# A transpose of the identity ahead of each run of products by weights, in a two-layer decoder trunk

## The chip, the cores and the metric

The kernel runs on one core of a Trainium2 chip. The metric is the device time of one execution in microseconds (us), lower is better; the time of a kernel is the median of its runs. A core has five engines with a queue each: TensorE (PE in the profile; its weight loads stand apart as PEld), VectorE (DVE), ScalarE (ACT), GpSimd (POOL) and SyncE (SP), which here only issues transfers. TensorE writes its results to PSUM, eight banks of which the kernel uses as one pool.

## The reference

The model is a decoder trunk of two layers over 256 tokens of width 2048. Each layer has a token mixer and a SwiGLU feed-forward network (FFN). Layer 0 mixes by retention with 8 heads, layer 1 by a short gated convolution. Cut to what matters here:

```python
for i in range(DEPTH):                                  # DEPTH = 2
    mod = (c_act @ w_mod[i] + b_mod[i])[:, None, :]
    sh1, sc1, g1, sh2, sc2, g2 = jnp.split(mod, 6, axis=-1)
    h = rms_norm(x, norm1_g[i]) * (1.0 + sc1) + sh1
    y = retention_mixer(h, ...) if i == 0 else short_conv_mixer(h, ...)
    x = x + g1 * y
    h = rms_norm(x, norm2_g[i]) * (1.0 + sc2) + sh2
    a, b = jnp.split(h @ ffn_w_in[i], 2, axis=-1)       # 2048 -> 2 x 5632
    x = x + g2 * ((silu(a) * b) @ ffn_w_out[i])         # 5632 -> 2048
return rms_norm(x, final_g)
```

Nearly all the arithmetic is in products of 256 tokens by weight matrices in 32-bit floats, 7296 tiles of 128 x 128 weights in all.

## The kernel before

**Splitting.** A 32-bit number is carried as two parts, `hi` (the number cast to the type `fp32r` that TensorE multiplies quickly) and `lo` (what the cast left out). A product of weights by activations is made of three terms: `hi` by `hi`, `hi` by `lo` and `lo` by `hi`. The activations lie in SBUF with both parts side by side, 2 x 256 columns, so that one matmul by `hi` weights does two terms.

**Weights.** They lie in one array in the order of use. Each transfer (`fetch`) brings 128 x 2048 numbers, 1 MB. `prepare` splits a half of that, 1024 columns or eight tiles of 128: ACT casts `hi` (L323), DVE subtracts to get `lo` (L326). Four such halves have room. `take` hands out the next tile and prepares up to two halves ahead.

**Products.** Most tiles pass through `product` (L356 to L374). For each tile it issues a pair: a 512-wide matmul of `hi` by both parts of the activations (L368), and a 256-wide one of `lo` by the upper part (L371). In each group all tiles of a column add up in one bank. 5396 pairs run in all: 496 in the retention's output (`rm` in the profile), the others in the FFNs and the convolution (`h` on the way in, `mid` on the way out). `packed` (L376) uses three 256-wide matmuls per tile, `tokens` (L402 to L420) 512-wide ones with the activations as the stationary side; both are used in the retention, `packed` also for the last column of an `output`.

**Order.** TensorE's queue has the order in which the code is written (a manual schedule). A scheduler places the instructions of DVE and ACT, outside the opening, by priorities. The stages on TensorE are: the retention's projections and heads, with the two halves of its output (`ret_out`) after four heads each; then FFN 0, the convolution, FFN 1. `normed` opens each of these last three: it works on six columns with 258-wide matmuls (L552 to L554) while the norm is computed. Then runs of `product` follow without a break, the input columns and `output` (L576) for the way out. In an FFN two such rounds come one after the other, 1994 pairs between `normed` and the last, `packed` column; in the convolution 912 pairs.

**Asides.** The last head before each `ret_out` leaves two pieces of work for later: `outputs` (nine 512-wide matmuls, L918) after 6 tiles, and `turned` (eight transposes of 128 x 128, L937) after 26 more or as soon after as the tiles of a row allow. They fall among the first pairs of `ret_out`.

Of the kernel before, what the change touches and what calls it, by code (L numbers as in the profile page):

```python
# [17 lines left out]
P = 128  # L18
# [28 lines left out]
MOST = 0.045  # L47
MOD_PRIO = -300
STEPS = (6, 26)
RAW_BUFS = 3  # L50
PART_BUFS = 4
ROW_AT = 64
# [146 lines left out]
def trunk(ctx: ExitStack, tc: tile.TileContext, x_in, c_in, pos_in, w_mod, cols_in, tab_in, w_all, out):  # L199
    nc = tc.nc  # L200
# [7 lines left out]
    def name(s):  # L208
        serial[0] += 1
        return f"{s}_{serial[0]}"  # L210

    def tmp(tag, shape=(P, S), dtype=F32, pool=work, bufs=None):
        return pool.tile(list(shape), dtype, tag=tag, name=name(tag), bufs=bufs)
# [24 lines left out]
    inv_freq, ident = tab[:, 0:1], tab[:, 1 : 1 + P]  # L238
# [7 lines left out]

    def mod_raw(t, pool=wpool, bufs=RAW_BUFS):
        raw = pool.tile([P, CHUNK], F32, tag="raw", name=name("raw"), bufs=bufs)
        nc.sync.dma_start(raw, w_mod[t])
        return raw  # L250
# [29 lines left out]
    def paced(n):  # L280

        units[0] += n
        due = 0
        for (a, i), (b, j) in zip(plan_mod, plan_mod[1:]):
            if units[0] >= a:
                due = min(j, i + (units[0] - a) * (j - i) // (b - a))
        allowed[0] = min(allowed[0] + n * MOST, 2.0) if n <= 64 else 0.0
        while todo and n_mod - len(todo) < due and allowed[0] >= 1.0:
            allowed[0] -= 1.0
            modulation(*todo.pop())  # L290

    def needed(layer, which, last=KT - 1):
        while any(m[:2] == (layer, which) and m[2] <= last for m in todo):
            modulation(*todo.pop())
# [7 lines left out]
    def fetch():  # L302
        raw = wpool.tile([P, CHUNK], F32, tag="raw", name=name("raw"), bufs=RAW_BUFS)
        nc.sync.dma_start(raw, w_all[n_fetched[0]])
        n_fetched[0] += 1
        fetched.append(raw)

    def prepare(between=None):
# [5 lines left out]
        if i == 0:  # L314
            if not fetched:
                fetch()
            raws[:] = [fetched.pop(0)]
            while first <= units[0] < early and len(fetched) < RAW_BUFS - 1 and n_fetched[0] < w_all.shape[0]:
                fetch()
# [11 lines left out]
    def take(group, k, col, width=P):  # L331

        assert order.pop() == (group, k, col, width)
        i = taken_cols[0] % HALF
        if i == 0:
            if ready and taken_cols[0]:
                ready.pop(0)
            while len(ready) < 1 + AHEAD * (units[0] >= first):
                n = len(ready)
                prepare()  # L340
                if len(ready) == n:
                    break
        taken_cols[0] += width
        return [t[:, i : i + width] for t in ready[0]]

    def bank():
        return ps.tile([P, 2, S], F32, tag="bank", name=name("bank"))

    asides, since = [], [0]

    def ticked(n):

        since[0] += n
        if asides and since[0] >= asides[0][0]:
            asides.pop(0)[1]()
            since[0] = 0  # L356

    def product(g, act, base=0, before=None, banks=None, last=True):

        fresh = not banks  # L360
        banks = banks or [bank() for _ in g.cols]
        for k in g.ks:
            if before:
                before(k)
            h = act[k - base]
            for c, pt in zip(g.cols, banks):
                hi, lo = take(g, k, c)
                nc.tensor.matmul(  # L368
                    pt, hi, h, start=fresh and k == g.ks[0], stop=False, skip_group_check=True
                )  # L370
                nc.tensor.matmul(  # L371
                    pt[:, 1, :], lo, h[:, 0, :], start=False, stop=last and k == g.ks[-1], skip_group_check=True
                )
            ticked(len(g.cols))  # L374
        paced(len(g.cols) * len(g.ks))
        return banks  # L376
# [87 lines left out]
    def norm_sums(accs):  # L464

        pt = bank()
        for i, acc in enumerate(accs):
            for t in range(2):
                nc.tensor.matmul(
                    pt[:, 0, t : t + 1], acc[:, t * P : (t + 1) * P], ones[:, 0:1],  # L470
                    start=i + t == 0, stop=i == len(accs) - 1, skip_group_check=True,
                )
        return pt

    def norm_roots(pt, n):

        r = tmp("rs", (P, 2), bufs=4)
        nc.vector.tensor_scalar(r, pt[:, 0, 0:2], 1.0 / n, EPS, op0=ALU.mult, op1=ALU.add)
        r2 = tmp("rs", (P, 2), bufs=4)
        nc.gpsimd.tensor_tensor(r2, r, half, op=ALU.pow)  # L480
        return r2
# [27 lines left out]
    def modulated(h, j, rb, layer, norm):  # L509
        shifted(h, scaled(j, rb, layer, norm), j, layer, norm)  # L510
# [18 lines left out]
    def normed(accs, layer, norm, g):  # L529

        needed(layer, SH2 if norm else SH1)
        shift = mod_s[layer][norm].unsqueeze(2).to_broadcast([P, KT, 2])
        ends = [h_open[:, :, i, S:] for i in range(2)]
        nc.scalar.copy(ends[0], shift)
        nc.vector.tensor_tensor(ends[1], shift, ends[0].bitcast(F32), op=ALU.subtract)
        banks = [bank().rearrange("p a b -> p (a b)")[:, : S + 2] for _ in g.cols]  # L540
        made = [0]

        def more(n):
            while made[0] < n:
                modulated(h[made[0]], made[0], root, layer, norm)
                made[0] += 1

        for k in g.ks:
            rows = [h_open[:, k, i, :] for i in range(2)]
            for c, pt in zip(g.cols, banks):  # L550
                hi, lo = take(g, k, c)
                nc.tensor.matmul(pt, hi, rows[0], start=k == 0, stop=False)  # L552
                nc.tensor.matmul(pt, hi, rows[1], start=False, stop=False)  # L553
                nc.tensor.matmul(pt, lo, rows[0], start=False, stop=k == KT - 1)  # L554
            if k == ROOTS_AT:
                r = norm_roots(norm_sums(accs), D)
            elif k == SPREAD_AT:
                root = tmp("rb", bufs=1)
                nc.scalar.copy(root, norm_spread(r))
            elif k > SPREAD_AT:  # L560
                more(min(k, made[0] + 2))
        more(KT)
        paced(len(g.cols) * len(g.ks))

        def total(pt, dst=None):
            end = tmp("end", (P, 1), bufs=2)
            nc.scalar.copy(end, pt[:, S : S + 1])
            t = tmp("low", bufs=3)
            nc.vector.tensor_tensor(t, pt[:, :S], root, op=ALU.mult)
            dst = tmp("sum", bufs=4) if dst is None else dst  # L570
            nc.scalar.activation(dst, t, AF.Identity, bias=end)
            return dst

        return [lambda dst=None, pt=pt: total(pt, dst) for pt in banks]

    def output(groups, act, which, last, after=None, base=None):  # L576

        layer, gate = which[0], mod_g[which[0]][which[1] == GT2]
        first, *groups = groups
        base, acc = first.ks[0] if base is None else base, None  # L580
        banks = product(first, act, base, last=False)
        for j, g in enumerate(groups):
            needed(*which, j)
            col = gate[:, j : j + 1]
            if last and j == KT - 1:
                (pt,) = packed(g, act, base)
                nc.vector.scalar_tensor_tensor(x[j], pt[:, 0, :], col, x[j], op0=ALU.mult, op1=ALU.add)
                acc = [acc, squares(None, x[j], "acc1")]
                if after:
                    after(j)  # L590
                return acc
            (pt,) = product(g, act, base, banks=banks[j : j + 1])
            t = tmp("sum", bufs=4)
            nc.vector.scalar_tensor_tensor(t, pt[:, 1, :], col, x[j], op0=ALU.mult, op1=ALU.add)
            nc.vector.scalar_tensor_tensor(x[j], pt[:, 0, :], col, t, op0=ALU.mult, op1=ALU.add)
            if last:
                acc = squares(acc, x[j])
            if after:
                after(j)


    with ExitStack() as inner:
# [70 lines left out]
        fresh = set()  # L673

        with tc.tile_pool(name="start", bufs=1) as sp:
# [57 lines left out]
            with tc.manual_schedule(engines={mybir.EngineType.DVE, mybir.EngineType.Activation}):  # L733
# [58 lines left out]
                banks = [bank() for _ in range(8)]  # L792

                def before(k):
                    low = []
                    prepare(lambda: low.append(row(k)))
                    low[0]()
# [109 lines left out]
        def mixed(head, both, v, sg):  # L907
# [36 lines left out]

            return list(zip(STEPS, [outputs, turned]))

# [39 lines left out]
    def sums(g):  # L986
        (pt,) = product(g, h)
        return lambda dst=None: summed(pt, dst)
# [108 lines left out]
```

## Time and profile before

| | us |
|---|---|
| Median of 3 runs | 2659.72 (2659.34 to 2661.05) |
| The profiled execution | 2657.39 |
| Its span | 2655.50 |
| Chain that ended last: PE | 76% of the span |
| Chain that ended last: "issue" | 20% of the span |
| DMA: read from HBM | 682.99 MB, 258 GB/s over the span |

The profile is of one execution. A group of instructions has a count, a total busy time and a mean duration. TensorE's matmuls are pipelined: a new one starts before the recorded end of the one before it. The recorded 399 ns of an L368 and 281 ns of an L371 therefore add up to more than the time that a pair takes, which has to be read from the starts. "Issue" in the chain of work is time for which the profile shows nothing that the engine waited for.

### The profile page before, as it was taken

How to read it: one execution, taken by the hardware profiler on the slowest of the kernel's cores; microseconds unless marked ns; L12 is line 12 of the kernel's file. 1: busy time of each engine (PE TensorE's matmuls, PEld its weight loads, DVE VectorE, ACT ScalarE, POOL GpSimd, SP SyncE). 2: the span in 40 equal slices, each digit the busy share in tenths (PEclk: the TensorE clock that was granted, in tenths of full speed). 3: DMA queues.
4: the chain of work that ended last, by engine and by line, in shares of the span. 5: the costliest groups of instructions: out<-in, count | busy, mean ns of one | idle time of the engine just before them, and what ended most of it. 6: DMA issues, size and time to landing. Idle time of an engine off the chain costs nothing.

```text
span 2655.5 us, 38222 instructions
## 1 busy us (share of the span) xinstructions
PE 2623.5 (99%) x15220; PEld 2298.5 (87%) x15220; DVE 1988.7 (75%) x2526; ACT 1245.2 (47%) x1755; POOL 148.3 (6%) x230
## 2 busy tenths in 40 slices
PE   7999999999999999999999999999999999999998
PEld 5998889888899888888888898888988888888887
DVE  7988878787798777777777888888886665555554
ACT  5545443444455444344444454444554443444443
POOL 0000001110000011101000001100000000000000
PEclk9999999999999999999999999999999999999999
DMA  9976668787687777777777768777676665555553
GB/s 398 401 270 242 238 232 319 267 301 263 244 301 260 295 285 271 279 276 280 273 279 262 279 214 328 276 276 257 254 278 247 252 222 183 183 190 190 181 185 126
DMA packets 96950, 687.58 MB, mean 259 GB/s; under 512 B 10753, under 2 KB 12545, under 8 KB 13825
## 3 DMA queue, kind: packets, MB, share of 16 engines
q1 hardware_dynamic: 96194, 684.48, 70.0%
q8 instruction: 119, 1.95, 0.3%
q10 hardware_dynamic: 576, 0.66, 0.1%
q14 instruction: 61, 0.50, 0.1%
HBM read 682.99 MB, written 2.10 MB: 258 GB/s over the span
## 4 chain that ended last, share of the span: by engine, by line
PE 76%; issue 20%; DVE 2%; DMA 1%; ACT 0%; SPq 0%; POOL 0%; POOLq 0%; ACTq 0%; DVEq 0%
PE bank L368 35%; PE bank L371 18%; PE bank L406 4%; PE bank L407 4%; PE bank L408 4%; PE bank L393 1%; PE bank L392 1%; PE bank L391 1%; PE bank L553 1%; PE bank L552 1%; PE bank L554 1%; DMA raw<-w_all 1%; PE bank L436 1%; PE bank L435 1%; PE bank L434 1%
## 5 line engine op out<-in xcount | busy, mean ns | idle before, releaser
L326 DVE TENSOR_TENSOR lo<-raw,hi 128x1024 fp32r<-128x1024 f32 x912 | 1111.4, 1223 | 573.9 <-ACT hi L323 571.3
L323 ACT CAST hi<-raw 128x1024 fp32r<-128x1024 f32 x912 | 953.1, 1049 | 1127.3 <-PE bank L368 653.3
L368 PE MATMUL bank<-h,hi 128*128 128x512 f32 x3296 | 1164.8, 399 | 0.0
L371 PE MATMUL bank<-h,lo 128*128 128x256 f32 x3296 | 925.7, 281 | 0.0
L368 PEld LDWEIGHTS bank<-h,hi 128*128 128x128 f32 x3296 | 619.3, 188 | 154.4
L371 PEld LDWEIGHTS bank<-h,lo 128*128 128x128 f32 x3296 | 622.6, 189 | 0.0
L368 PE MATMUL bank<-mid,hi 128*128 128x512 f32 x1604 | 566.0, 398 | 0.0
L371 PE MATMUL bank<-mid,lo 128*128 128x256 f32 x1604 | 450.5, 281 | 0.5 <-DVE lo L326 0.5
L257 DVE SCALAR_TENSOR_TENSOR raw<-raw,cb 128x2048 f32<-128x2048 f32 x160 | 365.6, 2285 | 12.9 <-DMA raw<-w_mod 12.8
L368 PEld LDWEIGHTS bank<-mid,hi 128*128 128x128 f32 x1604 | 301.2, 188 | 74.3
L371 PEld LDWEIGHTS bank<-mid,lo 128*128 128x128 f32 x1604 | 303.0, 189 | 0.8 <-DVE lo L326 0.8
L406 PE MATMUL bank<-hi,h 128*128 128x512 f32 x512 | 201.6, 394 | 0.0
L407 PE MATMUL bank<-lo,h 128*128 128x512 f32 x512 | 201.0, 393 | 0.0
L408 PE MATMUL bank<-hi,h 128*128 128x512 f32 x512 | 200.2, 391 | 0.0
L368 PE MATMUL bank<-rm,hi 128*128 128x512 f32 x496 | 172.8, 395 | 0.0
L371 PE MATMUL bank<-rm,lo 128*128 128x256 f32 x496 | 137.7, 278 | 0.0
L408 PEld LDWEIGHTS bank<-hi,h 128*128 128x128 f32 x512 | 96.7, 189 | 20.8
L406 PEld LDWEIGHTS bank<-hi,h 128*128 128x128 f32 x512 | 96.8, 189 | 17.7
L368 PEld LDWEIGHTS bank<-rm,hi 128*128 128x128 f32 x496 | 93.0, 188 | 21.7
L407 PEld LDWEIGHTS bank<-lo,h 128*128 128x128 f32 x512 | 96.9, 189 | 17.1
L371 PEld LDWEIGHTS bank<-rm,lo 128*128 128x128 f32 x496 | 93.2, 188 | 0.2
L267 POOL TENSOR_TENSOR g<-msum,cols 128x1 f32<-128x1 f32 x64 | 34.9, 545 | 949.0 <-DVE raw L257 939.0
(159 smaller groups left out, 2459.4 us busy)
## 6 DMA issues: line engine op xcount, KB each, us to landing
raw<-w_all SPq DMA_DIRECT2D x456, 1024.0 KB, 4.9
raw<-w_mod SPq DMA_DIRECT2D x192, 1024.0 KB, 5.1
x<-x_in SPq DMA_DIRECT2D x4, 512.0 KB, 5.6
decay<-tab_in SPq DMA_DIRECT2D x8, 128.0 KB, 3.3
out<-out SPq DMA_DIRECT2D x4, 256.0 KB, 3.2
out<-out ACTq DMA_DIRECT2D x3, 128.0 KB, 2.7
out<-out SPq DMA_DIRECT2D x1, 384.0 KB, 2.6
out<-out ACTq DMA_DIRECT2D x1, 256.0 KB, 3.2
```

What stands on the lines that cost most here:

```text
L257: nc.vector.scalar_tensor_tensor(raw, raw, 1.0, cb, op0=ALU.mult, op1=ALU.mult, accum_out=total)
L267: nc.gpsimd.tensor_tensor(dst, total, b, op=ALU.add)
L323: nc.scalar.copy(hi, raw)
L326: nc.vector.tensor_tensor(lo, raw, hi.bitcast(F32), op=ALU.subtract)
L368: nc.tensor.matmul(pt, hi, h, start=fresh and k == g.ks[0], stop=False, skip_group_check=True)
L371: nc.tensor.matmul(pt[:, 1, :], lo, h[:, 0, :], start=False, stop=last and k == g.ks[-1], skip_group_check=True)
L391: nc.tensor.matmul(pt, hi, h[:, 0, :], start=first, stop=False, skip_group_check=True)
L392: nc.tensor.matmul(pt, hi, h[:, 1, :], start=False, stop=False, skip_group_check=True)
L393: nc.tensor.matmul(pt, lo, h[:, 0, :], start=False, stop=last, skip_group_check=True)
L406: nc.tensor.matmul(flat(pt), a[:, 0, :], hi, start=first, stop=False)
L407: nc.tensor.matmul(flat(pt), a[:, 0, :], lo, start=False, stop=False)
L408: nc.tensor.matmul(flat(pt), a[:, 1, :], hi, start=False, stop=last)
```

## The change

`product` gets one more instruction in some of its calls. When it opens fresh banks and a counter `due_gap` is zero or less, it transposes the 128 x 128 identity (`ident`, which lies in the tile `tab`) into the first 128 columns of its first bank. The first pair into this bank starts it anew (`start=True`), so nothing of the transpose remains. The counter is then set to 384 and goes down by the number of pairs that each call issues. `normed` and `output` set it to zero, so the next `product` call in fresh banks opens with a transpose.

```diff
+GAP_EVERY = 384
...
-    asides, since = [], [0]
+    asides, since, due_gap = [], [0], [0]
...
         fresh = not banks
         banks = banks or [bank() for _ in g.cols]
+        if fresh and due_gap[0] <= 0:
+            nc.tensor.transpose(banks[0][:, 0, :P], ident, ident)
+            due_gap[0] = GAP_EVERY
+        due_gap[0] -= len(g.cols) * len(g.ks)
         for k in g.ks:
...
+        due_gap[0] = 0
         for k in g.ks:
             rows = [h_open[:, k, i, :] for i in range(2)]
...
         first, *groups = groups
+        due_gap[0] = 0
         base, acc = first.ks[0] if base is None else base, None
         banks = product(first, act, base, last=False)
```

This makes 17 transposes. Two stand ahead of the halves of `ret_out`. In each FFN there are six: the first after `normed`, the others after 384, 224, 384, 384 and 288 more pairs, with 330 pairs behind the last. In the convolution there are three: after `normed`, after 384 and after 288 more pairs, with 240 behind the last. The changed kernel's lines lie 5 to 7 further on: its pair is L373 and L376, `normed` L558 to L560, and the transpose L364.

On TensorE, where `normed` of FFN 0 ends (L552 to L554, 258 wide) and the pairs begin, there stands before (`bank`, `lo`, `hi` and `h` are the tiles of the text above, with serial numbers):

```order
L552 MATMUL bank_7246<-h,hi_7567 128x258
L553 MATMUL bank_7246<-h,hi_7567 128x258
L554 MATMUL bank_7246<-h,lo_7568 128x258
L368 MATMUL bank_7727<-h,hi_7601 128x512
L371 MATMUL bank_7727<-h,lo_7602 128x256
```

and now:

```order
L558 MATMUL bank_7248<-h,hi_7569 128x258
L559 MATMUL bank_7248<-h,hi_7569 128x258
L560 MATMUL bank_7248<-h,lo_7570 128x258
L364 MATMUL bank_7729<-tab 128x128
L373 MATMUL bank_7729<-h,hi_7603 128x512
L376 MATMUL bank_7729<-h,lo_7604 128x256
```

The transpose is the one row that is new, and it writes the bank of the pairs behind it.

Where the scheduler moves something on DVE, it looks like this, at the first columns of FFN 0 behind `normed`. Before (`sum` and `m` finish a column, `raw,msum` is a modulation product, `lo` prepares weights):

```order
L326 TENSOR_TENSOR lo_7836<-raw_7833,hi_7835 128x1024
L326 TENSOR_TENSOR lo_7856<-raw_7833,hi_7855 128x1024
L445 TENSOR_TENSOR sum_7826<-bank_7770,low_7824 128x256
L257 SCALAR_TENSOR_TENSOR raw_7875,msum_7877<-raw_7875,cb 128x2048
L1005 TENSOR_TENSOR m_7828<-sum_7826,silu_7822 128x256
L326 TENSOR_TENSOR lo_7884<-raw_7881,hi_7883 128x1024
```

and now:

```order
L327 TENSOR_TENSOR lo_7839<-raw_7836,hi_7838 128x1024
L450 TENSOR_TENSOR sum_7829<-bank_7773,low_7827 128x256
L258 SCALAR_TENSOR_TENSOR raw_7878,msum_7880<-raw_7878,cb 128x2048
L1012 TENSOR_TENSOR m_7831<-sum_7829,silu_7825 128x256
L327 TENSOR_TENSOR lo_7859<-raw_7836,hi_7858 128x1024
```

The second `lo` has moved behind a sum, a modulation product and an `m`. Some 18 rows of DVE and 11 of ACT stand elsewhere in this way, in FFN 0, the convolution and FFN 1; SP and POOL keep their order.

## The prediction

> **What bounds the kernel now.** I start with the page's shares and its strip of 40 slices, to see which engine fills the span.
>
> ```profile
> PE 2623.5 (99%) x15220; PEld 2298.5 (87%) x15220; DVE 1988.7 (75%) x2526; ACT 1245.2 (47%) x1755; POOL 148.3 (6%) x230
> PE   7999999999999999999999999999999999999998
> ```
>
> PE is busy nearly from end to end. Next the waits: of PE for others over the whole run, and of the others from 700 to 2640 us (engine and line, what was waited for: us in total, times, longest).
>
> ```profile
> PE bank L436 <- DVE lo L326: 6.2, 5, 2.2
> ...
> PE bank L371 <- DVE lo L326: 0.5, 1, 0.5
> ...
> ACT hi L323 <- PE bank L368: 624.5, 403, 4.6
> ```
>
> The largest of PE's waits comes to 6.2 us and belongs to the opening (L436). The pairs of `product` (L368 and L371) wait 0.5 us, once. The weight preparation, on the other hand, waits 624.5 us for PE to give buffers back. So the time is the number of PE's matmuls times the spacing of their starts. A busy share of 99% does not say whether that spacing is the best one, since the recorded durations overlap. Hence I asked for the first and last start of L368, the first matmul of a pair, in stretches where only pairs run (group xcount: duration ns min/median/max, first and last start us, forms).
>
> ```profile
> L368 PE MATMUL bank<-rm,hi x209: 392/392/395, 359.9 to 432.0; 128*128 128x512 f32 x105
> L368 PE MATMUL bank<-rm,hi x195: 392/392/395, 705.7 to 772.9; 128*128 128x512 f32 x195
> L368 PE MATMUL bank<-mid,hi x148: 391/391/391, 1833.8 to 1884.7; 128*128 128x512 f32 x148
> ...
> L368 PE MATMUL bank<-h,hi x1312: 392/398/403, 817.5 to 1405.0; 128*128 128x512 f32 x188
> L368 PE MATMUL bank<-mid,hi x682: 395/398/403, 1032.3 to 1521.6; 128*128 128x512 f32 x171
> ...
> L368 PE MATMUL bank<-h,hi x672: 393/398/403, 1565.9 to 1803.0; 128*128 128x512 f32 x168
> L368 PE MATMUL bank<-mid,hi x80: 395/398/403, 1803.4 to 1831.3; 128*128 128x512 f32 x80
> ...
> L368 PE MATMUL bank<-h,hi x1312: 393/398/403, 1929.6 to 2517.2; 128*128 128x512 f32 x188
> L368 PE MATMUL bank<-mid,hi x682: 395/398/403, 2144.5 to 2633.8; 128*128 128x512 f32 x171
> ```
>
> **Two paces of the same pair.** In the first three rows a pair takes (432.0 - 359.9)/208 = 346.6 ns, 67.2/194 = 346.4 ns and 50.9/147 = 346.3 ns; the starts are rounded to 0.1 us, so I use 346.6. In the others it takes (1521.6 - 817.5)/1993 = 353.3 ns in the first FFN (1312 + 682 = 1994 pairs), (1831.3 - 1565.9)/751 = 353.4 ns in the convolution (752 pairs) and (2633.8 - 1929.6)/1993 = 353.3 ns in the second FFN (1994 pairs). No other value appears over a long stretch, and neither pace drifts. The difference is 6.7 ns.
>
> Is this the clock, or a neighbour's load? The windows view sets a quick stretch beside a slow one (window: length, then busy time of PE, PEld, DVE, ACT and POOL, granted clock, DMA share, GB/s).
>
> ```profile
> 358.50:432.00 73.50, 73.50 (x427) 64.21 (x426) 59.13 (x72) 27.42 (x28) 3.48 (x8) 1.00 0.75 274
> 820.00:1519.00 699.00, 699.00 (x3958) 606.18 (x3957) 530.75 (x634) 321.80 (x455) 55.36 (x78) 1.00 0.76 280
> ```
>
> The clock is 1.00 in both, the DMA share 0.75 and 0.76, and DVE is even busier in the quick one (59.13/73.50 = 80%, against 76%). What differs is the rhythm of the starts, and what came ahead of it. The timeline shows the slow rhythm, and one change to the quick (start us, us, engine and line, tiles, count).
>
> ```profile
> 1200.11 0.40 PE L368 MATMUL bank<-h,hi 128*128 128x512 f32 x1
> ...
> 1200.46 0.40 PE L368 MATMUL bank<-h,hi 128*128 128x512 f32 x1
> ...
> 1200.82 0.40 PE L368 MATMUL bank<-h,hi 128*128 128x512 f32 x1
> ...
> 1201.17 0.40 PE L368 MATMUL bank<-h,hi 128*128 128x512 f32 x1
> ...
> 357.25 0.40 PE L368 MATMUL bank<-rm,hi 128*128 128x512 f32 x1
> 357.49 0.28 PE L371 MATMUL bank<-rm,lo 128*128 128x256 f32 x1
> 357.61 1.04 PE L937 MATMUL bank<-tab,o 128*128 128x128 f32 x8
> 358.40 0.48 PE L368 MATMUL bank<-rm,hi 128*128 128x512 f32 x1
> 358.72 0.28 PE L371 MATMUL bank<-rm,lo 128*128 128x256 f32 x1
> 358.83 0.40 PE L368 MATMUL bank<-rm,hi 128*128 128x512 f32 x1
> ```
>
> In the slow rhythm the steps are 0.35, 0.36, 0.35 and so on: three pairs take 1.06 us. From 357.61 eight transposes (L937) go by, and the pairs behind them are the quick row from 359.9 on. The same happens at 704 us, ahead of the row from 705.7. Only these two groups of transposes in the trace are followed by pairs, and both times the pace is quick up to the end of the run, for about 200 pairs. The third quick stretch began at the one stall, 0.48 us for a `lo`:
>
> ```profile
> 1832.51 0.39 PE L371 MATMUL bank<-mid,lo 128*128 128x256 f32 x1 [0.48 <-DVE lo L326]
> ```
>
> Behind `normed`'s 258-wide matmuls, which is where the two FFNs and the convolution begin, the pace was slow three times in three. My reading, which no row proves: a stream of pairs settles in a rhythm at its first matmuls and keeps it until something breaks it. A wide matmul hands it on without a gap; a transpose, only 128 columns wide, leaves TensorE's stream empty for a moment, as a stall does, and the next pairs start in the quick rhythm.
>
> **The change part by part.** It adds 17 transposes: two ahead of the halves of `ret_out`, three behind `normed`, five ahead of the `output` stages of FFN and convolution, seven inside a run, each 384 pairs after the one before.
>
> Cost: from L368 at 357.25 to L368 at 358.83 are 1.58 us for two pairs and eight transposes; 1.58 - 2 x 0.353 = 0.87 us, that is 0.109 us each, the longer first pair behind them (358.40 to 358.83) included. 17 x 0.109 = **+1.9 us**, all on PE's path.
>
> ```profile
> L937 PE MATMUL bank<-tab,o x64: 270/272/273, 238.9 to 704.9; 128*128 128x128 f32 x64
> ```
>
> This row holds all 64 transposes of the trace; the last one starts at 704.9 us. A single transpose may pay that first pair alone: 0.43 - 0.35 = 0.08 us more, so at most 17 x 0.19 = 3.2 us; the lower end is nothing. I take 1.9, as its row is the same operation at the same place.
>
> The Trainium skill, "TensorE: Matmul & The Clock Gate", Part 4, gives some 275 ns for a 128x128 transpose inside a kernel, and says that transposes do not count as busy for the clock gate. The row above records 272 ns for one (the median of the 64), but eight of them delay the stream by 0.109 us each, and the granted clock in the stretch behind them is 1.00; by the page's figure the added cost would be 17 x 0.275 = 4.7 us, an estimate.
>
> Gain: the slow pairs behind the third transpose are 1994 + 752 + 1994 = 4740. At 6.7 ns each, **-31.8 us**. The first two transposes come 6 pairs ahead of the attention's own 512-wide matmuls (L918). Behind those run 30 pairs up to the L937 group:
>
> ```profile
> 347.01 0.39 PE L368 MATMUL bank<-rm,hi 128*128 128x512 f32 x1
> ...
> L368 PE MATMUL bank<-rm,hi x30: 393/398/403, 347.0 to 357.2; 128*128 128x512 f32 x30
> ```
>
> From 347.01 to 357.25 these 30 took 10.24/29 = 353.1 ns each, the slow pace again. So a new stream of wide matmuls decides there, and I count no gain; the two halves hold 36 such pairs each, at most 72 x 6.7 ns = 0.5 us.
>
> Waits: a transpose takes over the wait for its bank from the first pair, so nothing new is waited for. PE running 2% quicker asks for weights sooner. What covers that is the 624.5 us that ACT stands waiting for PE's buffers, most of all in the FFNs. The scheduler also puts seven `lo` splits of DVE a few places later; the longest thing that can slip ahead of one is a modulation product:
>
> ```profile
> L257 DVE SCALAR_TENSOR_TENSOR raw<-raw,cb 128x2048 f32<-128x2048 f32 x160 | 365.6, 2285 | 12.9 <-DMA raw<-w_mod 12.8
> ```
>
> Where the cover is gone, as at 1832.51, one such slip costs up to 2.3 us. I take nothing, and keep +2.3 for the upper end and -0.5 (that stall gone) for the lower. DMA queues keep their order, and what is late next is again PE.
>
> Sum: -31.8 + 1.9 = -29.9 us. The profiled execution took 2657.39 us (its span 2655.50 and 1.89 around it) and would become 2627.5. It lies 2.3 us under the median of the runs shown, 2659.72, so the median becomes **2629.8 us**. Own range of this case: down to 2659.7 - 31.8 - 0.5 - 0.5 = 2626.9, up to 2629.8 + 1.3 + 2.3 = 2633.4.
>
> **The rivals.** (1) The transpose does break the rhythm, but in both directions: what meets a slow stream leaves it quick, what meets a quick one leaves it slow. For it: no row shows a transpose behind quick pairs. Against it: eight in a row, an even number, turned slow into quick twice. With runs of 384, 224, 384, 384, 288 and 330 pairs in an FFN every second one would be quick, 384 + 384 + 288 = 1056 per FFN, and 384 + 80 of the slow ones in the convolution: 2576 pairs x 6.7 ns = 17.3 us, less 1.9: 2659.7 - 15.4 = **2644.3 us**. Other mixtures, such as openings that do not take, lie between 2634 and 2655.
>
> (2) One transpose is not enough; it takes a drained stream, as a group of eight or a stall leaves. For it: single ones don't occur in the trace. Against it: at 1832.51 one gap of half a microsecond was enough, and each transpose of the group is spaced like the next. Nothing is gained, 2659.7 + 1.9 = **2661.6 us**, 0.07% more, which is no change.
>
> (3) The other side: one transpose leaves the stream in a third rhythm, in which each pair takes the longest step of the slow one, 0.36 us (1200.46 to 1200.82). Its place is the same 4740 pairs, its price 6.7 ns on each: 31.8 + 1.9, **2693 us**. It decides from some 510 pairs on, (5.3 - 1.9)/0.0067, where 5.3 us is 0.2% of the time. Against it: no long stretch of the trace has that pace.
>
> **How the numbers follow.** Forecast 0.64; rival 1 with the mixtures 0.16; rival 2 0.13; rival 3 0.07. What weighs most is that three disturbances of the pairs by emptiness led to the quick pace and five by wide matmuls to the slow one; what holds me back is that one transpose alone, and one behind quick pairs, are not in the trace. A measurement of this kernel can tell about 0.2%, 5.3 us, from no change. The forecast and rival 1 lie more than that below: faster 0.80; same 0.13; slower 0.07. The range takes in the forecast with its bounds and the mixtures, 2626.5 to 2655, and leaves out rivals 2 and 3, 0.20.
>
> **What would show it.** Right: first and last starts of the pairs' first matmul give 346 to 347 ns in all FFN and convolution stretches; the first FFN's 1994 pairs take about 691 us instead of 704; a transpose moves its successors by about 0.11 us; PE's waits stay under 3 us there; the granted clock stays at 1.00. Wrong in rival 1: the pace alternates from transpose to transpose. In rival 2 it is 353.3 throughout. In rival 3 a pace of about 360 appears. My step on waits is wrong if PE's waits for `lo` or `hi` grow by more than a few us in the convolution.

## The result, and the profile after

The changed kernel took 2629.81 us in the median of four runs (2627.45 to 2631.77), against 2659.53 us before (2656.91 to 2661.05, four runs). The ratio is 0.9889, with a 95% interval of 0.9872 to 0.9906. The forecast was 2629.8 us. The span of the profiled execution went from 2655.5 to 2628.0 us.

The profiled execution of the changed kernel, from its page:

```profile
span 2628.0 us, 38255 instructions
...
PE 2595.0 (99%) x15237; PEld 2293.7 (87%) x15237; DVE 1986.6 (76%) x2526; ACT 1244.7 (47%) x1755; POOL 152.5 (6%) x230
```

The shares are nearly those of before, 99% for PE in both, though the time is 1.1% shorter. This is why busy shares could not show the gain: the engine was as busy at the slower pace. The starts of the pairs' first matmul show it. These are the groups of L373 in the changed kernel for FFN 0, the convolution and FFN 1 (count, duration ns, first and last start us):

```profile
L373 PE MATMUL bank<-h,hi x1312: 391/391/476, 819.8 to 1396.8; 128*128 128x512 f32 x188
L373 PE MATMUL bank<-mid,hi x682: 392/395/480, 1030.8 to 1511.4; 128*128 128x512 f32 x171
...
L373 PE MATMUL bank<-h,hi x672: 391/391/476, 1555.7 to 1788.5; 128*128 128x512 f32 x168
L373 PE MATMUL bank<-mid,hi x240: 389/391/480, 1788.9 to 1873.1; 128*128 128x512 f32 x120
...
L373 PE MATMUL bank<-h,hi x1312: 391/391/476, 1915.3 to 2492.3; 128*128 128x512 f32 x188
L373 PE MATMUL bank<-mid,hi x682: 392/395/480, 2126.3 to 2606.8; 128*128 128x512 f32 x171
```

FFN 0 takes 1511.4 - 819.8 = 691.6 us from its first pair to its last, against 704.1 before; FFN 1 takes 691.5 against 704.2. Per pair that is 691.6/1993 = 347.0 ns with the five transposes inside, and 346.7 without them. The convolution needs a row of before that covers all of its 912 pairs:

```profile
L368 PE MATMUL bank<-h,hi x672: 393/398/403, 1565.9 to 1803.0; 128*128 128x512 f32 x168
L368 PE MATMUL bank<-mid,hi x240: 391/391/403, 1803.4 to 1887.5; 128*128 128x512 f32 x120
```

It went from 321.6 to 317.4 us. Its one stall, for the same `lo` split, grew:

```profile
1818.12 0.38 PE L376 MATMUL bank<-mid,lo 128*128 128x256 f32 x1 [1.04 <-DVE lo L327]
```

The three stages gave 12.5 + 4.2 + 12.7 = 29.4 us, but the span only 27.5. The retention ahead of them took 2.3 us longer: the first pair of FFN 0 starts at 819.8 instead of 817.5. What follows FFN 1's last pair was 0.5 us shorter (21.2 instead of 21.7 us). The timeline of the changed kernel shows where most of the 2.3 us arose, at the first `ret_out`, behind the 512-wide matmuls L925 (L918 before), and the windows view of 346.9 to 350.4 us shows why, first of before, then of the changed kernel (length, busy time of each engine, granted clock, DMA share, GB/s):

```profile
348.38 0.63 PE L373 MATMUL bank<-rm,hi 128*128 128x512 f32 x1
...
349.02 0.63 PE L373 MATMUL bank<-rm,hi 128*128 128x512 f32 x1
...
349.66 0.63 PE L373 MATMUL bank<-rm,hi 128*128 128x512 f32 x1
```

```profile
346.90:350.40 3.50, 3.50 (x21) 3.02 (x20) 1.60 (x4) 1.68 (x3) 0.69 (x1) 1.00 0.03 11
```

```profile
346.90:350.40 3.50, 3.50 (x12) 2.85 (x11) 0.19 (x2) 1.35 (x3) 0.69 (x1) 0.52 0.22 82
```

For about 3.4 us the granted clock was half, and a pair took 0.64 us there. PE had just waited for the attention's operands, as it does before, too. Of the kernels below some show this window and some don't, with the same code at this place (`three_ahead` does and `three_behind` doesn't), so it does not take the change's transposes to bring it. Comparing single spans to better than about 2 us is pointless for that reason; the stages are compared instead.

### The profile page after: what moved, and what is told of

It is laid out like the page before. It is cut to its first block, busy times and chain, and to the rows that moved or that the text cites. A ratio compares the mean times of both kernels' runs of the same rounds, so it can differ in the third digit from the quotient of the medians.

```text
span 2628.0 us, 38255 instructions
## 1 busy us (share of the span) xinstructions
PE 2595.0 (99%) x15237; PEld 2293.7 (87%) x15237; DVE 1986.6 (76%) x2526; ACT 1244.7 (47%) x1755; POOL 152.5 (6%) x230
## 4 chain that ended last, share of the span: by engine, by line
PE 75%; issue 20%; DVE 2%; DMA 2%; ACT 0%; POOL 0%; POOLq 0%; SPq 0%; ACTq 0%; DVEq 0%
PE bank L373 34%; PE bank L376 18%; PE bank L411 4%; PE bank L412 4%; PE bank L413 4%; DMA raw<-w_all 2%; PE bank L398 1%; PE bank L397 1%; PE bank L396 1%; PE bank L559 1%; PE bank L558 1%; PE bank L560 1%; PE bank L441 1%; PE bank L440 1%; PE bank L439 1%
## 5 line engine op out<-in xcount | busy, mean ns | idle before, releaser
L373 PE MATMUL bank<-h,hi 128*128 128x512 f32 x3296 | 1143.9, 391 | 0.0
L376 PE MATMUL bank<-h,lo 128*128 128x256 f32 x3296 | 922.7, 280 | 0.0
L373 PEld LDWEIGHTS bank<-h,hi 128*128 128x128 f32 x3296 | 616.4, 187 | 134.9
L376 PEld LDWEIGHTS bank<-h,lo 128*128 128x128 f32 x3296 | 622.9, 189 | 0.0
L373 PE MATMUL bank<-mid,hi 128*128 128x512 f32 x1604 | 556.8, 394 | 0.0
L376 PE MATMUL bank<-mid,lo 128*128 128x256 f32 x1604 | 444.9, 277 | 1.0 <-DVE lo L327 1.0
L373 PEld LDWEIGHTS bank<-mid,hi 128*128 128x128 f32 x1604 | 300.7, 187 | 69.2
L376 PEld LDWEIGHTS bank<-mid,lo 128*128 128x128 f32 x1604 | 301.3, 188 | 1.4 <-DVE lo L327 1.4
L413 PE MATMUL bank<-hi,h 128*128 128x512 f32 x512 | 200.2, 391 | 0.0
L373 PE MATMUL bank<-rm,hi 128*128 128x512 f32 x496 | 173.9, 396 | 0.0
L376 PE MATMUL bank<-rm,lo 128*128 128x256 f32 x496 | 138.0, 278 | 0.0
L413 PEld LDWEIGHTS bank<-hi,h 128*128 128x128 f32 x512 | 96.7, 189 | 20.8
L373 PEld LDWEIGHTS bank<-rm,hi 128*128 128x128 f32 x496 | 93.6, 189 | 22.2 <-DVE sum L450 0.3
L376 PEld LDWEIGHTS bank<-rm,lo 128*128 128x128 f32 x496 | 93.6, 189 | 0.1
```

The source lines that it names most:

```text
L373: nc.tensor.matmul(pt, hi, h, start=fresh and k == g.ks[0], stop=False, skip_group_check=True)
L376: nc.tensor.matmul(pt[:, 1, :], lo, h[:, 0, :], start=False, stop=last and k == g.ks[-1], skip_group_check=True)
L413: nc.tensor.matmul(flat(pt), a[:, 1, :], hi, start=False, stop=last)
```

## The experiments

Three questions were open. Is the quick rhythm kept or renewed by the repeats? Does only what stands directly ahead of the pairs count? And is it the empty stream that does it, as the prediction read it, the transpose as such, or something else? All kernels below leave out the two transposes at `ret_out` and all of those between `normed` and the next `normed`, unless it is said; what stands "in the three places" is directly behind `normed`. The common edit is

```diff
-GAP_EVERY = 384
+GAP_EVERY = 1 << 20
...
-    asides, since, due_gap = [], [0], [0]
+    asides, since, due_gap = [], [0], [GAP_EVERY]
...
         first, *groups = groups
-        due_gap[0] = 0
```

Paces are read from FFN 0, where in all but `three_ahead` the inserted instruction stands directly ahead of 1994 pairs that run to the end. Each pace comes from one profiled execution. But for `three_behind`, with four runs, each of these kernels was run once, so its time is a single value. In all kernels the convolution, up to the place in its output where the weights run late, and FFN 1 show the same pace as FFN 0: the same insertion gave the same rhythm three times in three.

**Only the three transposes (`three_behind`).** This is the common edit alone.

> Only the three transposes directly behind `normed` are kept, the other 14 are left out. Theory 'kept until broken' (a stream of pairs keeps its rhythm until something else comes in): all pairs behind the three transposes stay at 346.7 ns, each FFN's 1994 pairs take about 691.4 us, and the time is that of the changed kernel less 14 x 0.11 = 1.5 us, about 2628.3 us. Rival 'wears off' (the quick rhythm lasts only some hundred pairs and has to be renewed): quick for the first 400 to 1000 pairs of a stage, then 353.3 ns; 2635 to 2650 us.

The two groups of the pairs' first matmul in FFN 0:

```profile
L373 PE MATMUL bank<-h,hi x1312: 391/391/476, 817.6 to 1394.2; 128*128 128x512 f32 x188
L373 PE MATMUL bank<-mid,hi x682: 391/391/392, 1028.5 to 1508.6; 128*128 128x512 f32 x171
```

(1508.6 - 817.6)/1993 = 346.7 ns over the whole FFN: the rhythm does not wear off. The median was 2626.95 us, 0.990 of before with an interval of 0.9864 to 0.9936, which overlaps that of the full change. Three of its four runs took 2625.46 to 2627.03 us, the fourth 2644.69 us. The profile is of the shortest, so what held up the fourth is open; one FFN at the slow pace would account for 13.2 us of it. The traces tell the two kernels apart better: 691.0 us instead of 691.6 for the same pairs, so each of the five transposes inside FFN 0 costs 0.6/5 = 0.12 us and gains nothing.

**The three transposes ahead of `normed` (`three_ahead`).** Nothing stands behind `normed`; its first bank takes the transpose before its own first matmul.

```diff
-        due_gap[0] = 0
+        nc.tensor.transpose(banks[0][:, :P], ident, ident)
         for k in g.ks:
             rows = [h_open[:, k, i, :] for i in range(2)]
```

> The same three transposes, but ahead of the first matmul of `normed` instead of behind its last: 288 matmuls, 258 wide, now stand between each transpose and the pairs. Theory 'only what stands directly ahead counts': the pairs are at 353.3 ns throughout (but for what a stall changes in the convolution), FFN 0 takes 704.5 us from the first pair to the packed column, about 2660 us. Rival 'a transpose resets something that lasts': pairs at 346.7 ns, about 2628 us.

```profile
L373 PE MATMUL bank<-h,hi x1312: 392/398/403, 820.2 to 1407.8; 128*128 128x512 f32 x188
L373 PE MATMUL bank<-mid,hi x679: 395/398/403, 1035.0 to 1523.3; 128*128 128x512 f32 x170
```

703.1/1990 = 353.3 ns, and 2660.53 us: with the 288 matmuls of `normed` between the transpose and the pairs nothing is gained. It is no lasting reset.

**An ordinary matmul in the three places (`mm128`, `mm512`),** of parts of the activations in the pairs' own type, 128 and 512 wide. Where it stands, the edit is

```diff
-            nc.tensor.transpose(banks[0][:, 0, :P], ident, ident)
+            nc.tensor.matmul(banks[0][:, 0, :P], act[g.ks[0] - base][:, 0, :P],
+                             act[g.ks[0] - base][:, 0, :P], start=True, stop=True)
```

and for 512 wide the bank as a whole and both parts of the activations, `act[g.ks[0] - base]`.

> In the three places behind `normed` an ordinary matmul of two 128x128 parts of the activations, 128 wide, stands in place of the transpose. Theory 'emptiness' (a short instruction ahead of the pairs drains TensorE's stream): pairs at 346.7 ns, about 2628 us. Rival 'transpose mode' (only a transpose, which TensorE runs in another mode, changes the rhythm): pairs at 353.3 ns, about 2660 us.

> In the same three places an ordinary matmul 512 wide. Theory 'emptiness': it hands the stream on without a gap, so pairs at 353.3 ns, about 2660 us. Rival 'any matmul put in shifts the phase': pairs at 346.7 ns, about 2629 us. If the 128-wide one is quick and this one slow, the width decides; if both are slow, the transpose does; if both are quick, the phase does.

FFN 0 with 128 wide, then with 512 wide:

```profile
L373 PE MATMUL bank<-h,hi x1312: 393/398/447, 822.6 to 1410.2; 128*128 128x512 f32 x188
L373 PE MATMUL bank<-mid,hi x682: 395/398/403, 1037.5 to 1526.8; 128*128 128x512 f32 x171
```

```profile
L373 PE MATMUL bank<-h,hi x1312: 387/398/403, 822.0 to 1409.6; 128*128 128x512 f32 x188
L373 PE MATMUL bank<-mid,hi x681: 395/398/403, 1036.8 to 1525.8; 128*128 128x512 f32 x171
```

704.2/1993 and 703.8/1992 are both 353.3 ns; 2663.65 and 2661.14 us. As wide as the transpose, the ordinary matmul does nothing. That the instruction is narrow is therefore not enough. Three explanations were left: the transpose or a change of type counts, or the gap must be longer, or the exact offset decides.

**A plain f32 matmul, other widths, and wide matmuls inside a quick run.** The first is `matmul(banks[0][:, 0, :P], ident, ident, ...)`; the next two are the ordinary matmul with 64 and 256 columns. The last has transposes behind `normed` and an ordinary 512-wide matmul after every 384 pairs, 12 in all.

> As the run with three transposes, but in their place an ordinary 128x128 matmul of the identity by the identity in plain f32, neither transposed nor in the fp32r type of the pairs. Since an ordinary fp32r matmul of the same width left the pairs slow, width alone is out. Theory 'mode': leaving the pairs' own way of multiplying (fp32r) for another and coming back is what counts; then this is quick, 346.7 ns a pair, about 2628 us. Rival 'transpose only': slow, 353.3 ns, about 2660 us. Rival 'phase' (the rhythm depends on the exact offset at which the first pair starts, whatever made it) makes no sure forecast here.

> In the three places an ordinary fp32r matmul 64 wide, of the same type as the pairs. Theory 'mode': pairs at 353.3 ns, about 2660 us. Rival 'phase': a width of 64 ends at another offset than 128 or 512 (both slow); if the offset decides, one of the widths tried should be quick, 346.7 ns and about 2628 us.

> In the three places an ordinary fp32r matmul 256 wide. Theory 'mode': 353.3 ns, about 2660 us. Rival 'phase': a fourth offset, as with 64; quick would be 346.7 ns and about 2628 us.

> Transposes behind `normed` as in the run with three, so that each stage begins quick, and after every 384 pairs one ordinary fp32r matmul 512 wide. Theory 'kept until broken, and wide matmuls break it': the first 384 pairs of each stage at 346.7 ns, all later ones at 353.3 ns until a transpose or a stall; FFN 0 takes 133 + 1610 x 0.3533 = about 702 us, the whole about 2653 us. Rival 'only a change of mode moves it, in either direction': pairs stay at 346.7 ns, about 2630 us (12 matmuls of 0.23 us more than with three).

FFN 0 of the four, in this order:

```profile
L373 PE MATMUL bank<-h,hi x1312: 391/391/482, 817.1 to 1393.7; 128*128 128x512 f32 x188
L373 PE MATMUL bank<-mid,hi x682: 391/391/391, 1027.9 to 1508.1; 128*128 128x512 f32 x171
```

```profile
L373 PE MATMUL bank<-h,hi x1312: 391/391/474, 821.2 to 1397.8; 128*128 128x512 f32 x188
L373 PE MATMUL bank<-mid,hi x682: 391/391/391, 1032.0 to 1512.2; 128*128 128x512 f32 x171
```

```profile
L373 PE MATMUL bank<-h,hi x1312: 395/398/403, 821.8 to 1409.4; 128*128 128x512 f32 x188
L373 PE MATMUL bank<-mid,hi x681: 395/398/403, 1036.7 to 1525.7; 128*128 128x512 f32 x171
```

```profile
L378 PE MATMUL bank<-h,hi x1312: 390/391/476, 816.5 to 1394.1; 128*128 128x512 f32 x188
L378 PE MATMUL bank<-mid,hi x682: 390/391/397, 1027.6 to 1508.7; 128*128 128x512 f32 x171
```

The f32 matmul is quick, 691.0/1993 = 346.7 ns (2625.69 us). So is the 64-wide one, 346.7 ns (2629.59 us), though it is of the pairs' own type: neither the transpose nor a change of type is needed. The 256-wide one is slow, 703.9/1992 = 353.4 ns (2662.21 us). And the run with wide matmuls inside is quick, 692.2/1993 = 347.3 ns with five of them in FFN 0 (2627.27 us). Wide matmuls did not break a quick rhythm; the expectation that they would did not hold.

**Order by width, or not?**

> In the three places behind `normed` an ordinary fp32r matmul 32 wide. So far 64 wide was quick, 128, 256 and 512 wide were slow; the transpose and the f32 matmul were quick. Theory 'gap' (the matmul ahead must be so short that the stream stands empty for long enough before the first pair: the start behind it was recorded 28 to 29 ns on where it was quick, 58, 117 and 230 ns on where it was slow): quick, 346.7 ns, FFN 0's pairs in 691.3 us, about 2627 us. Rival 'phase' (an exact offset, with no order by width): either may come.

> The same, 96 wide, between the widest quick and the narrowest slow one. Theory 'gap': quick or slow, and it only narrows the bound; the start behind it should be recorded at some 40 to 45 ns. Rival 'phase': either. With 32 wide this shows whether the outcome is in order by width.

> In the three places two ordinary fp32r matmuls 128 wide, one behind the other. Theory 'gap': what stands directly ahead is the same as with one, so slow again, 353.3 ns, FFN 0's pairs in 704.5 us, about 2660 us. Rival 'phase': two of them shift the offset once more, so the outcome may turn to quick, about 2628 us. Quick here speaks against a bound on the gap before the first pair alone.

> In the three places a 64-wide fp32r matmul (quick by itself) and behind it one 512 wide, then the pairs. Theory 'only what stands directly ahead counts': slow, as with the 512-wide one alone, about 2660 us. Rival 'a quick state once entered outlives a wide matmul' (12 of 12 quick runs stayed quick across a 512-wide one): quick, 346.7 ns, about 2628 us.

FFN 0 with 32 wide, with 96 wide, with two 128 wide, and with 64 and then 512 wide:

```profile
L373 PE MATMUL bank<-h,hi x1312: 395/398/475, 817.4 to 1405.1; 128*128 128x512 f32 x188
L373 PE MATMUL bank<-mid,hi x682: 395/398/403, 1032.3 to 1521.7; 128*128 128x512 f32 x171
```

```profile
L373 PE MATMUL bank<-h,hi x1312: 391/391/459, 816.8 to 1393.4; 128*128 128x512 f32 x188
L373 PE MATMUL bank<-mid,hi x682: 391/391/391, 1027.7 to 1507.8; 128*128 128x512 f32 x171
```

```profile
L374 PE MATMUL bank<-h,hi x1312: 395/398/445, 820.0 to 1407.7; 128*128 128x512 f32 x188
L374 PE MATMUL bank<-mid,hi x682: 395/398/403, 1034.9 to 1524.3; 128*128 128x512 f32 x171
```

```profile
L374 PE MATMUL bank<-h,hi x1312: 392/394/395, 819.3 to 1395.8; 128*128 128x512 f32 x188
L374 PE MATMUL bank<-mid,hi x682: 392/394/395, 1030.1 to 1510.2; 128*128 128x512 f32 x171
```

32 wide is slow (704.3/1993 = 353.4 ns), 96 wide quick (691.0, 346.7 ns), two of 128 slow (704.3), 64 and then 512 quick (690.9, 346.7 ns). The times were 2656.80, 2625.31, 2660.99 and 2628.17 us.

| directly behind `normed` | time per pair in FFN 0, ns |
|---|---|
| nothing (before) | 353.3 |
| ordinary, 32 wide | 353.4 |
| ordinary, 64 wide | 346.7 |
| ordinary, 96 wide | 346.7 |
| ordinary, 128 wide, one or two | 353.3, 353.4 |
| ordinary, 256 and 512 wide | 353.4, 353.3 |
| 64 wide, then 512 wide | 346.7 |
| plain f32, 128 wide | 346.7 |
| transpose, 128 wide | 346.7 |

A difference of 0.1 ns in this table lies within the rounding of the starts. The outcome is not in order by width, so no single bound on the width, or on a gap that goes by the width, sorts it. At the recorded starts the 32-wide and the 64-wide kernel can hardly be told apart (timeline of each, first pairs of FFN 0):

```profile
817.39 0.18 PE L364 MATMUL bank<-h 128*128 128x32 f32 x1
817.42 0.47 PE L373 MATMUL bank<-h,hi 128*128 128x512 f32 x1
817.73 0.28 PE L376 MATMUL bank<-h,lo 128*128 128x256 f32 x1
...
818.20 0.40 PE L373 MATMUL bank<-h,hi 128*128 128x512 f32 x1
...
818.56 0.40 PE L373 MATMUL bank<-h,hi 128*128 128x512 f32 x1
```

```profile
821.15 0.19 PE L364 MATMUL bank<-h 128*128 128x64 f32 x1
821.18 0.47 PE L373 MATMUL bank<-h,hi 128*128 128x512 f32 x1
821.49 0.28 PE L376 MATMUL bank<-h,lo 128*128 128x256 f32 x1
...
821.96 0.39 PE L373 MATMUL bank<-h,hi 128*128 128x512 f32 x1
...
822.31 0.39 PE L373 MATMUL bank<-h,hi 128*128 128x512 f32 x1
```

Both have 0.03 us from the insertion to the first pair and 0.31 us to its second matmul, and yet one stays slow for 1994 pairs and the other quick. The third pair starts 0.78 us behind the first in both; only from there on do they part, with 0.36 us to the next pair in the one and 0.35 us in the other. What decides cannot be seen at the 10 ns of this view.

**Late weights** in the convolution's output speak the same way. The 128-wide kernel waited 0.78 us there for a `lo`, and these are its pairs behind that wait:

```profile
L373 PE MATMUL bank<-mid,hi x154: 392/398/403, 1838.4 to 1892.4; 128*128 128x512 f32 x154
```

54.0/153 = 352.9 ns, slow still. Five kernels with a slow stream show a wait there: in two the pace turned quick behind it (before and `three_ahead`), in three it stayed slow (`mm128`, `mm256`, `two_mm128`). In `mm512` and `mm32`, which show no wait of PE there, it turned quick at the same place. The six with a wait in a quick stream (the changed kernel, `fp32_128`, `mm64`, `wide_inside`, `mm96` and `mm64_512`) were all quick behind it.

**The transposes at `ret_out`.** The changed kernel has two more transposes ahead of pairs that were not running yet. They stand behind the 512-wide matmuls of `tokens` (L413) instead of `normed`'s 258-wide ones. Its timeline at the first:

```profile
340.08 0.27 PE L364 MATMUL bank<-tab 128*128 128x128 f32 x1
...
340.54 0.40 PE L373 MATMUL bank<-rm,hi 128*128 128x512 f32 x1
...
341.60 0.40 PE L373 MATMUL bank<-rm,hi 128*128 128x512 f32 x1
```

The three pairs from 340.54 to 341.60 take 1.06 us, as three slow pairs did in the prediction, and so do three at the second `ret_out` (691.97 to 693.03). Behind `normed` of the same kernel three take 1.04 us (820.22 to 821.26). Only six pairs follow each of these two transposes before the attention's matmuls, so how long the pace would last is not shown. But the same transpose was followed by quick pairs three times in three behind `normed` and by slow ones two times in two here: the inserted instruction alone does not decide.

## Why the prediction was right, and where it was not

- **What bounds the kernel** held: PE's starts set the time. PE's waits in `product` went from 0.5 to 1.0 us, well under the 3 us that the prediction allowed.
- **Two paces, and the pairs that change over** held. 4740 pairs were named, and in FFN 0, the convolution and FFN 1 all of them run at 346.7 ns.
- **The cost of a transpose** was put at 0.109 us; 0.12 was measured. One alone is about as cheap as one of eight. The estimate of 4.7 us for the 17, by the figure of some 275 ns in the Trainium skill, "TensorE: Matmul & The Clock Gate", Part 4, did not come: 17 x 0.12 = 2.0 us.
- **The sum** was -29.9 us and the medians differ by 29.7. For an FFN the working gives 1994 x 6.7 ns - 5 x 0.109 = 12.8 us, and 12.5 and 12.7 were measured. The convolution gave 4.2 against 752 x 6.7 ns - 0.2 = 4.8, since its stall grew by 0.56 us. The half-clock window at 347 us was not in the sum; three pairs at 0.64 instead of 0.353 us are 0.9 us of it alone. So the profiled execution was forecast at 2627.5 us and took 2629.79. That the medians agree with the sum to 0.2 us is partly luck: the runs of either kernel lie some 4 us apart.
- **Rival 1** fell in the changed kernel itself: transposes met quick streams twelve times, and all twelve runs stayed quick. **Rival 2** fell: behind `normed` one is enough. **Rival 3** did not appear.
- **The reading of the mechanism was wrong in one step.** The prediction had it that a narrow instruction "leaves TensorE's stream empty for a moment, as a stall does, and the next pairs start in the quick rhythm", and counted the stall of before as a third witness. Behind a 128-wide matmul, as narrow as the transpose, and behind a 32-wide one, which the first pair follows as soon as it does the 64-wide one, the pairs stay slow. Three of five stalls in slow streams leave them slow as well. The number came out right because it rested on the two groups of eight transposes, the same operation, and not on the reading. That a single one behind `normed` would do as well was in no row of before, and the prediction gave it no more than 0.64. It was in part luck: of the eight single instructions tried in that place four give the quick pace and four the slow one.
- "Wide matmuls hand on the slow rhythm" was half right: behind `normed` and the attention they lead into it, but inside a quick run they leave it as it is.

What is shown: the pairs keep one of two paces, and a single instruction between `normed` and the pairs is enough to choose it. The quick pace outlived everything tried within a stage (transposes, 512-wide matmuls, stalls). The slow one ended at some stalls and not at others. Each insertion behind `normed` gave one outcome in all three stages of its profiled execution. What is not settled is what makes the choice. An exact offset of a few ns at the first pair is one reading that is left; no run set or measured such an offset.

For the kernel: in the profiled execution three transposes do all that the 17 do. That version is not told apart from the change by its median (2626.95 against 2629.81 us), but by 0.6 us in FFN 0.

## What to carry to other kernels

When PE is busy 99% and waits for nobody, divide first and last starts by the count, stage by stage. If the same sequence runs at two paces in one trace, look at what stood ahead of each stretch before looking for a neighbour's load. The price of an operation that the trace already shows can be taken over, here 0.109 us against 0.12 measured. A story of why it works needs its own test, and here a matmul of the same width was enough to upset it.

## What was not expected of the hardware

A stream of alternating 512- and 256-wide fp32r matmuls holds one of two paces, 346.7 or 353.3 ns a pair, for up to 1994 pairs without drifting, at a granted clock of 1.00. Behind 258-wide matmuls a single fp32r matmul ahead of the stream can choose which one, in no order by its width: 32 slow, 64 and 96 quick, 128, 256 and 512 slow. A transpose was followed by the quick pace there, and by the slow one behind 512-wide matmuls. And the attention's waits of PE at the first `ret_out`, 1.7 and 0.9 us long, were in some executions followed by some 3.4 us at half the granted clock, with a pair at 0.64 us (6.8 us of half clock in `mm512`), and in others not.
